# An encoder layer on one core: slots, orders at the seams, and own buffers for a head's first keys

## The chip, the cores and the metric

The kernel runs on one core of a Trainium2 chip. A core has the engines PE (matrix products), DVE, ACT and POOL (elementwise work) and SP, which here issues the DMAs. The metric is the device time of one execution in microseconds (us); less is better.

## The reference

One layer of a bidirectional encoder over 1024 positions of width 1024, in fp32:

```python
h   = rms_norm(x, g_pre)
z   = h @ W_in            # q, f_fwd, f_bwd, i, gate | u, v | two merge gates
A   = hgrn2(q, f_fwd, f_bwd, i) * silu(gate)     # 8 heads of 128 keys, both directions
Bm  = gelu(u) * (W_s @ layer_norm(gelu(v)) + b)  # per chunk of 128 positions
mix = (sigmoid(gate_a) * (A @ W_a) + sigmoid(gate_b) * (Bm @ W_b)) @ W_out
x   = x + rms_norm(mix, g_post)
x   = x + rms_norm(swiglu(rms_norm(x, g_ffn)), g_ffn_post)   # hidden width 2816
x   = x + (p @ W_ple) * sigmoid(x @ W_ple_gate)
```

In a head, S_t = diag(f_t) S_(t-1) + k_t v_t^T and o_t = S_t^T q_t, forward and backward, with f = lb + (1 - lb) sigmoid(zf) and k = (1 - lb) sigmoid(-zf).

## The kernel before

Every fp32 operand of a large product is split into a high and a low part (split_into: ACT writes the high part, DVE or POOL the low one), and each product is made in three passes (mm3, mm3c). A product on PE covers 128x512 of the output. Activations stay in SBUF with the features on the partitions; halves of 512 positions (n) are the unit.

The stages follow each other. First p @ W_ple (ple_product), while x is normalised and transposed to hT (norm_x, to_fm). Then four token-major groups (tm_group) make v, i and u, a spatial gate acts on u, and u is transposed to bT. branch_b multiplies w_b by bT, and beside it DVE forms the sums T1 to T4 of the four quarters of hT. These feed the class Seven, which makes a product of 2x2 blocks from seven block products (for the columns of q, gate and the merge, and later for the FFN's gate and up; begin makes the first two of the seven ahead). Then come the eight heads. For a head, proj multiplies two blocks of weights by hT and makes F (decays), X and Y (keys); scores goes through the levels m = 1, 2, 4, ..., 64. At each level PE makes scores of QA and X for both halves, DVE multiplies QA and X by F and puts the scores into SC (merge), and POOL renews Y; outputs chains the states S through the chunks on DVE and makes the head's output. The loop issues proj of the next head ahead of outputs of the current one. merge multiplies the heads' outputs by w_a, mix_half multiplies by W_out and normalises (y), and to_fm1 transposes for the FFN, which ends with down and the gated residual.

A scheduler with a timeline of its own sets each engine's order from the dependencies; the source order decides what it can see when. Each tile has a tag in a pool with a number of buffers, and an instruction that writes a buffer waits for the last readers of what was there. PSUM has eight banks under the tags mm (3), sc (2), tr, st and o. Loads are issued on SP in order, so a load whose buffer is not free holds those behind it.

## Time and profile before

| | |
|---|---|
| median of 3 runs | 1989.25 us (1988.0 to 1991.34) |
| profiled execution | 1992.11 us, span 1990.3 us |
| PE busy | 1926.7 us, 97% |
| DVE, ACT, POOL busy | 1106.0, 764.9, 208.5 us |
| mean granted clock of PE | 0.989 |

The span runs from the first to the last instruction of the trace. Busy time counts an engine's instructions; a product that runs at the lower clock counts as busy for longer. The stages by the trace: the start to 53 us, the other token-major groups to 229, the transposes of u and w_b's products to about 284, Seven's columns to about 560, the heads to 1037, the merge to about 1115, W_out and the norm to about 1220, the FFN and the end to 1990.

### The profile page before, as it was taken

How to read it: one execution, taken by the hardware profiler on the slowest of the kernel's cores; microseconds unless marked ns; L12 is line 12 of the kernel's file. 1: busy time of each engine (PE TensorE's matmuls, PEld its weight loads, DVE VectorE, ACT ScalarE, POOL GpSimd, SP SyncE). 2: the span in 40 equal slices, each digit the busy share in tenths (PEclk: the TensorE clock that was granted, in tenths of full speed). 3: DMA queues.
4: the chain of work that ended last, by engine and by line, in shares of the span. 5: the costliest groups of instructions: out<-in, count | busy, mean ns of one | idle time of the engine just before them, and what ended most of it. 6: DMA issues, size and time to landing. Idle time of an engine off the chain costs nothing.

```text
span 1990.3 us, 24039 instructions
## 1 busy us (share of the span) xinstructions
PE 1926.7 (97%) x9264; PEld 1604.8 (81%) x9264; DVE 1106.0 (56%) x1694; ACT 764.9 (38%) x1434; POOL 208.5 (10%) x153
## 2 busy tenths in 40 slices
PE   7999899999998999999999998999999999999999
PEld 6887788888887888888877886888888888888887
DVE  6401357545247777788754457855555536545743
ACT  7211244344344555445542146533333324213321
POOL 2600000000012222222112101000000000001000
PEclk9999899999999999999998998999999999999999
DMA  9120155433130112211336223232222205324232
GB/s 339 57 70 11 59 175 179 138 110 118 70 138 32 59 59 69 69 59 59 107 110 229 98 94 117 84 100 92 75 85 77 83 32 197 106 74 158 87 105 80
DMA packets 82147, 201.87 MB, mean 101 GB/s; under 512 B 8688, under 2 KB 17520, under 8 KB 82032
## 3 DMA queue, kind: packets, MB, share of 16 engines
q1 hardware_dynamic: 82032, 200.33, 30.0%
q8 instruction: 73, 1.20, 0.3%
q14 instruction: 42, 0.34, 0.1%
HBM read 147.35 MB, written 52.95 MB: 101 GB/s over the span
## 4 chain that ended last, share of the span: by engine, by line
PE 55%; DVE 5%; ACT 3%; issue 1%; DMA 1%; POOL 0%; DVEq 0%; SPq 0%; ACTq 0%; POOLq 0%
PE ps_mm L133 17%; PE ps_mm L280 12%; PE ps_sc L133 8%; PE ps_sc L280 6%; PE ps_st L133 4%; PE ps_sc L612 2%; DVE QA L621 1%; PE ps_tr L280 1%; PE ps_o L280 1%; PE ps_st L280 1%; DVE X L624 1%; PE ps_o L700 1%; DVE SC L634 1%; DVE F L654 1%; ACT SC L631 1%
## 5 line engine op out<-in xcount | busy, mean ns | idle before, releaser
L280 PE MATMUL ps_mm<-T,w 128*128 128x512 f32 x1296 | 310.1, 389 | 0.0
L280 PEld LDWEIGHTS ps_mm<-T,w 128*128 128x128 f32 x1296 | 243.2, 188 | 50.7 <-ACT u L230 0.2
L648 POOL TENSOR_TENSOR Y<-X,F 128x512 f32<-128x512 f32 x56 | 92.7, 1656 | 675.6 <-DVE F L587 401.8
L115 DVE TENSOR_TENSOR whl<-raw,whl 128x1024 fp32r<-128x1024 f32 (+1 forms) x70 | 85.5, 1225 | 132.0 <-ACT whl L114 132.0
L612 PE MATMUL ps_sc<-QA,X 128*128 128x128 f32 x896 | 125.5, 290 | 19.7 <-DVE QA L621 17.1
L115 DVE TENSOR_TENSOR w<-sums,w 128x1024 fp32r<-128x1024 f32 x72 | 88.1, 1223 | 92.8 <-ACT w L114 92.7
L612 PEld LDWEIGHTS ps_sc<-QA,X 128*128 128x128 f32 x896 | 115.1, 194 | 27.7 <-DVE QA L621 10.5
L133 PE MATMUL ps_mm<-whl,act 128*128 128x512 f32 x528 | 134.1, 389 | 0.0
L114 ACT ACTIVATE whl<-raw 128x1024 fp32r<-128x1024 f32 (+1 forms) x78 | 79.0, 1014 | 115.3 <-PE ps_sc L133 54.0
L133 PE MATMUL ps_mm<-hTa,whl 128*128 128x512 f32 x480 | 119.2, 396 | 0.0
L133 PE MATMUL ps_mm<-hTb,whl 128*128 128x512 f32 x480 | 117.8, 398 | 0.5 <-ACT F L580 0.5
L133 PEld LDWEIGHTS ps_mm<-whl,act 128*128 128x128 f32 x528 | 99.1, 188 | 20.7
L114 ACT ACTIVATE w<-sums 128x1024 fp32r<-128x1024 f32 x72 | 76.0, 1056 | 98.2 <-PE ps_sc L280 80.6
L280 PE MATMUL ps_sc<-T,w 128*128 128x512 f32 x432 | 108.5, 389 | 0.0
L621 DVE TENSOR_TENSOR QA<-QA,F 128x512 f32<-128x512 f32 x112 | 85.8, 767 | 34.1 <-PE ps_sc L612 33.5
L133 PEld LDWEIGHTS ps_mm<-hTb,whl 128*128 128x128 f32 x480 | 89.0, 189 | 18.7 <-ACT F L580 1.3
L133 PEld LDWEIGHTS ps_mm<-hTa,whl 128*128 128x128 f32 x480 | 88.4, 188 | 17.6 <-ACT F L580 0.2
L280 PEld LDWEIGHTS ps_sc<-T,w 128*128 128x128 f32 x432 | 81.1, 188 | 16.8
L133 PE MATMUL ps_sc<-whl,act 128*128 128x512 f32 x351 | 89.8, 390 | 0.0
L133 PEld LDWEIGHTS ps_sc<-whl,act 128*128 128x128 f32 x351 | 65.7, 188 | 13.8 <-ACT acc L927 0.2
L624 DVE TENSOR_TENSOR X<-X,F 128x256 f32<-128x256 f32 x112 | 74.6, 699 | 0.1
L645 ACT ACTIVATE X<-Y 128x512 f32<-128x512 f32 x56 | 36.1, 645 | 99.0 <-PE ps_sc L612 95.4
(311 smaller groups left out, 3566.7 us busy)
## 6 DMA issues: line engine op xcount, KB each, us to landing
raw<-in_w_fm_dram SPq DMA_DIRECT2D x52, 512.0 KB, 3.5
raw<-in_w_gate_dram SPq DMA_DIRECT2D x22, 512.0 KB, 3.4
raw<-in_w_up_dram SPq DMA_DIRECT2D x22, 512.0 KB, 3.9
act_d<-s SPq DMA_DIRECT2D x22, 512.0 KB, 2.9
raw<-in_w_down_dram SPq DMA_DIRECT2D x22, 512.0 KB, 3.8
raw<-act_d SPq DMA_DIRECT2D x22, 512.0 KB, 4.2
raw<-in_w_tm_dram SPq DMA_DIRECT2D x16, 512.0 KB, 5.6
pr_d<-h SPq DMA_DIRECT2D x16, 256.0 KB, 5.9
```

The lines of the kernel that those rows point to most:

```text
L114: nc.scalar.activation(hi, src, AF.Copy)
L115: (eng or nc.vector).tensor_tensor(out=lo, in0=src, in1=hi.bitcast(F32), op=ALU.subtract)
L133: nc.tensor.matmul(ps, lhsT=lhs(lp, k), rhs=rhs(rp, k), start=(i == 0), stop=(i == n - 1))
L280: nc.tensor.matmul(ps, lhsT=lhs(lp, k), rhs=rhs(rp, k), start=(first and i == 0), stop=(i == n - 1), skip_group_check=True)
L612: nc.tensor.matmul(sp[:, i * P:(i + 1) * P], lhsT=X[:, c * P:(c + 1) * P], rhs=view(QA, c * P, [[2 * m, cb], [T + m, 2], [1, m]]), start=T ...
L621: nc.vector.tensor_tensor(out=view(QA, o, qd), in0=view(QA, o, qd), in1=view(F, of + 1, [[nb - 1, 2], [2, nb // 4], [0, m]]), op=ALU.mult)
L624: nc.vector.tensor_tensor(out=view(X2, o, dims), in0=view(X, o, dims), in1=view(F, nb + of + 1, [[4, nb // 8], [1 - nb, 2], [0, m]]), op=A ...
L631: nc.scalar.activation(SC[p0:p0 + m, 4 * g:4 * g + 4, c0:c0 + m], sp.rearrange("p (c t) -> p c t", c=4)[p0:p0 + m, :, c0:c0 + m], AF.Copy)
L634: nc.vector.copy_predicated(SC[:, 4 * g:4 * g + 4], masks[:, li, None, :].broadcast_to([P, 4, P]), sp.rearrange("p (c t) -> p c t", c=4))
L645: nc.scalar.activation(view(X2, m, mid), view(Y, m, mid), AF.Copy)
L648: nc.gpsimd.tensor_tensor(out=view(Y, m, mid), in0=view(X, m, mid), in1=view(F, 0, [[4, nb // 4], [nb + 3, 2], [0, m]]), op=ALU.mult)
L654: nc.vector.tensor_tensor(out=F2, in0=Fv[:, :, :, 0], in1=Fv[:, :, :, 1], op=ALU.mult)
```

## The change

to_fm no longer keeps fp32 copies of hT (h32); the sums T are made from the high and low parts (sum_of), with 40 adds instead of 24. The pools raw and whl are open from the start and are used by the token-major groups as well, in place of p0r and two of p0w's six buffers. The first halves of pT and w_ple are loaded in four pieces, ahead of x. bT is made before the fourth token-major group, as a pair for each half. The first keys of a head have a tag of their own, X0, with two buffers; those of the levels keep X with three. In the merge, blocks 0 and 1 of w_a are split before the last head's outputs, and block j + 2 is loaded ahead of block j's products and split behind them. At the FFN the second products of the first two blocks get the banks st and sc.

```diff
@@ -157,8 +157,6 @@
-                if keep[g] is not None:
-                    nc.scalar.activation(keep[g][:, :, col * P:(col + 1) * P], tv, AF.Copy)
...
@@ -234,12 +232,12 @@
-        def begin(self, lhs, HB):
+        def begin(self, lhs, HB, bank):
...
             c11 = self.keep("p1", X)
-            Z = self.zbank()
+            Z = ps_tile(bank)
             self.add(lhs, HB, 2, Z, True)
...
@@ -289,15 +287,14 @@
     c_p01, p01 = phase("p01", side="right")
-    c_h32, p_h32 = phase("h32", side="right")
-    h32 = [[p_h32.tile([P, 4, NH], F32, name=f"h32_{n}{g}") if n == 0 or g == 1 else None for g in range(2)]
-           for n in range(2)]
+    c_x, p0x = phase("p0x", 3, side="right")
+    c_raw, rawp = phase("raw", 2)
+    c_whl, whlp = phase("whl", 2)
     c_sgu, sgu = phase("sgu")
     masks = p01.tile([P, len(LEVELS), P], U8, name="masks")
-    c_x, p0x = phase("p0x", 3)
-    c_r, p0r = phase("p0r", 3)
-    c_w, p0w = phase("p0w", 6)
-    c_t, p0t = phase("p0t", 2)
+    c_v, p0v = phase("p0v", 4)
+    c_w, p0w = phase("p0w", 4)
+    c_t, p0t = phase("p0t", 1)
...
@@ -313,16 +310,24 @@
-    praw = [p0w.tile([P, 2, 2, NH], F32, name="praw", tag="whl") for _ in range(2)]
+    praw = [whlp.tile([P, 2, 2, NH], F32, name="praw", tag="whl") for _ in range(2)]
...
-    load_pw(0, 0)
+    def piece(i, cut):
+        src, w, raw = a[("pT", "w_ple")[i]][0][:, cut[0], cut[1]], pwt[i][:, 0], praw[i][:, 0, cut[0], cut[1]]
+        nc.sync.dma_start(raw, src)
+        split_into(w[:, 0, cut[0], cut[1]], w[:, 1, cut[0], cut[1]], raw)
+    both, all_ = slice(0, 2), slice(0, NH)
+    piece(0, (both, slice(0, P)))
+    piece(1, (slice(0, 1), all_))
+    piece(1, (slice(1, 2), all_))
+    piece(0, (both, slice(P, NH)))
     load_x(0)
-    load_pw(1, 0)
     nc.sync.dma_start(ident, a["ident"])
...
@@ -368,7 +372,7 @@
-            s = t2(p0t, "vs", 2)
+            s = t2(p0v, "vs", 4)
...
@@ -378,7 +382,8 @@
-        return load_split(a["w_tm"][gi, kk], [2, NH], nc.gpsimd if kk % 2 else nc.vector, p0w, p0r)
+        pool = p0w if (4 * gi + kk) % 6 < 4 else whlp
+        return load_split(a["w_tm"][gi, kk], [2, NH], nc.gpsimd if kk % 2 else nc.vector, pool, rawp)
...
@@ -393,7 +398,7 @@
-        s = h32[1][1][:, t % 4]
+        s = t2(p0v, "vs", 4)
...
@@ -443,22 +450,20 @@
                                        op0=ALU.add, op1=ALU.mult)
+    c_b, p1b = phase("p1b", side="right")
+    bT = [pair(p1b, f"bT{n}", None) for n in range(2)]
+    for t in range(NT):
+        tp = ps_tile(("tr", "o")[t % 2])
+        for i in range(4):
+            nc.tensor.transpose(tp[:, i * P:(i + 1) * P], u[:, t, i * P:(i + 1) * P], ident)
+        ts = slice(t % 4 * P, (t % 4 + 1) * P)
+        split_into(bT[t // 4][0][:, :, ts], bT[t // 4][1][:, :, ts], tp.rearrange("p (k t) -> p k t", k=4))
     w = [load_tm(3, kk) for kk in range(4)]
     tm_group(w, ev_i(1))
-    close(c_t, c_w, c_r, c_x)
-    c_b, p1b = phase("p1b", side="right")
-    bT = [p1b.tile([P, 4, T], F32R, name=f"bT{p}") for p in range(2)]
-    for t in range(NT):
-        tp = ps_any()
-        for i in range(4):
-            nc.tensor.transpose(tp[:, i * P:(i + 1) * P], u[:, t, i * P:(i + 1) * P], ident)
-        split_into(bT[0][:, :, t * P:(t + 1) * P], bT[1][:, :, t * P:(t + 1) * P],
-                   tp.rearrange("p (k t) -> p k t", k=4))
+    close(c_w, c_v)
     close(c_sgu)
-    c_raw, rawp = phase("raw", 2)
-    c_whl, whlp = phase("whl", 2)
     c_T, Tp = phase("hT_T")
...
@@ -472,7 +477,7 @@
             ps = ps_any()
-            mm3(ps, lambda p, k: wb[:, p, k, :], lambda p, k: bT[p][:, k, n * NH:(n + 1) * NH], 4)
+            mm3(ps, lambda p, k: wb[:, p, k, :], lambda p, k: bT[n][p][:, k, :], 4)
             s = t2(p1t, "o", 2)
...
@@ -480,23 +485,30 @@
-    b11, b21, b22 = h32[0][0], h32[0][1], h32[1][1]
-    b12 = [hT[1][p][0].bitcast(F32) for p in range(2)]
+    b11, b21 = [[hT[0][p][g].bitcast(F32) for p in range(2)] for g in range(2)]
+    b12, b22 = [[hT[1][p][g].bitcast(F32) for p in range(2)] for g in range(2)]
+    def sum_of(out, terms):
+        acc, sign = terms[0]
+        for term, sign in terms[1:]:
+            nc.vector.tensor_tensor(out=out, in0=acc, in1=term, op=ALU.add if sign else ALU.subtract)
+            acc = out
     for k in range(4):
         sa, sb = [st1.sum_tile().rearrange("p a k c -> p a (k c)") for _ in range(2)]
-        nc.vector.tensor_tensor(out=sa[:, 0], in0=b12[0][:, k], in1=b11[:, k], op=ALU.subtract)
-        nc.vector.tensor_tensor(out=sa[:, 0], in0=sa[:, 0], in1=b12[1][:, k], op=ALU.add)
+        (b11h, b11l), (b12h, b12l), (b21h, b21l), (b22h, b22l) = [
+            [part[:, k] for part in blk] for blk in (b11, b12, b21, b22)]
+        sum_of(sa[:, 0], [(b12h, 1), (b11h, 0), (b12l, 1), (b11l, 0)])
         split_into(T1[0][:, k], T1[1][:, k], sa[:, 0])
-        nc.vector.tensor_tensor(out=sa[:, 1], in0=b22[:, k], in1=sa[:, 0], op=ALU.subtract)
+        sum_of(sa[:, 1], [(b22h, 1), (sa[:, 0], 0), (b22l, 1)])
         split_into(T2[0][:, k], T2[1][:, k], sa[:, 1])
-        nc.vector.tensor_tensor(out=sb[:, 0], in0=b22[:, k], in1=b12[0][:, k], op=ALU.subtract)
-        nc.vector.tensor_tensor(out=sb[:, 0], in0=sb[:, 0], in1=b12[1][:, k], op=ALU.subtract)
+        sum_of(sb[:, 0], [(b22h, 1), (b12h, 0), (b22l, 1), (b12l, 0)])
         split_into(T3[0][:, k], T3[1][:, k], sb[:, 0])
-        nc.vector.tensor_tensor(out=sb[:, 1], in0=b21[:, k], in1=sa[:, 1], op=ALU.subtract)
+        sum_of(sb[:, 1], [(b21h, 1), (sa[:, 1], 0), (b21l, 1)])
         split_into(T4[0][:, k], T4[1][:, k], sb[:, 1])
...
         branch_b(j)
-    close(c_b, c_h32)
+    close(c_b)
...
@@ -565,7 +577,7 @@
-                s.X = hg.tile([P, T], F32, name="X", bufs=3)
+                s.X = hg.tile([P, T], F32, name="X0", bufs=2)
...
@@ -723,6 +735,16 @@
+    def load_wa(j):
+        raw = rawp.tile([P, KD, P], F32, name="raw", tag="raw")
+        nc.sync.dma_start(raw, a["w_a"][j])
+        return raw
+    def split_wa(raw):
+        w = whlp.tile([P, 2, KD, P], F32R, name="whl", tag="whl")
+        split_into(w[:, 0], w[:, 1], raw)
+        return w
     def gate_a(n):
...
@@ -746,6 +768,7 @@
             A1 = new_fm("A1")
+            wa = [split_wa(load_wa(j)) for j in range(2)]
         outputs(h, cur)
...
@@ -761,17 +784,20 @@
         for j in range(KD):
-            w = load_split(a["w_a"][j], [KD, P], None, whlp, rawp)
+            if j + 2 < KD:
+                raw = load_wa(j + 2)
             for n in range(2):
...
                 ps = ps_any()
-                mm3(ps, lambda p, k: w[:, p, k, :], fm_rhs(A[n]), KD)
-                sg = t2(t3, "sg", 2)
+                mm3(ps, lambda p, k: wa[j][:, p, k, :], fm_rhs(A[n]), KD)
+                sg = t2(t3, ("sg", "xr")[n], 2)
                 nc.sync.dma_start(sg, sig_d[j, :, ns])
...
                 nc.vector.tensor_tensor(out=M[:, j, ns], in0=sg, in1=m0, op=ALU.add)
+            if j + 2 < KD:
+                wa.append(split_wa(raw))
             load_wo(j)
...
@@ -860,9 +886,9 @@
-    begun = [st4.begin(lhs, HB2)]
+    begun = [st4.begin(lhs, HB2, "st")]
...
-    begun.append(st4.begin(lhs1, HB2))
+    begun.append(st4.begin(lhs1, HB2, "sc"))
```

PE has as many instructions as before, ACT 10 fewer, DVE 18 more, SP 2 more. In the order of PE, at the end of the fourth token-major group, the kernel before has the transposes of u (ident, u) behind the group's last products (hTb), and w_b's products (bT) behind these:

```order
L133 MATMUL ps_sc<-whl,hTb_144 128x512 x2
L133 MATMUL ps_sc<-whl,hTb_146 128x512
L456 MATMUL ps_mm<-ident,u 128x128 x4
L456 MATMUL ps_st<-ident,u 128x128 x4
L456 MATMUL ps_mm<-ident,u 128x128 x4
L456 MATMUL ps_sc<-ident,u 128x128 x4
L456 MATMUL ps_mm<-ident,u 128x128 x4
L456 MATMUL ps_sc<-ident,u 128x128 x4
L456 MATMUL ps_mm<-ident,u 128x128 x4
L456 MATMUL ps_st<-ident,u 128x128 x4
L133 MATMUL ps_mm<-bT_1611,whl 128x512
L133 MATMUL ps_mm<-bT_1612,whl 128x512
```

In the changed kernel two tiles of u stand there in the middle of that group, in its first half of positions (hTa):

```order
L133 MATMUL ps_sc<-whl,hTa_146 128x512 x2
L133 MATMUL ps_sc<-whl,hTa_148 128x512
L133 MATMUL ps_sc<-whl,hTa_146 128x512
L458 MATMUL ps_tr<-ident,u 128x128 x4
L458 MATMUL ps_o<-ident,u 128x128 x4
L133 MATMUL ps_sc<-whl,hTa_146 128x512
L133 MATMUL ps_sc<-whl,hTa_148 128x512
L133 MATMUL ps_sc<-whl,hTa_146 128x512 x2
L133 MATMUL ps_sc<-whl,hTa_148 128x512
L133 MATMUL ps_mm<-whl,hTa_145 128x512 x2
L133 MATMUL ps_mm<-whl,hTa_147 128x512
```

The other transposes stand in the same way ahead of the group's end, and the last product of the group is followed at once by w_b's:

```order
L133 MATMUL ps_sc<-whl,hTb_150 128x512 x2
L133 MATMUL ps_sc<-whl,hTb_152 128x512
L133 MATMUL ps_sc<-whl,hTb_150 128x512 x2
L133 MATMUL ps_sc<-whl,hTb_152 128x512
L133 MATMUL ps_mm<-bT_1375,whl 128x512
L133 MATMUL ps_mm<-bT_1376,whl 128x512
L133 MATMUL ps_mm<-bT_1375,whl 128x512 x2
L133 MATMUL ps_mm<-bT_1376,whl 128x512
```

In the order of PE where a new head begins, the kernel before has, between the first scores (q, ks) and the level m=1 (QA, X), products of projections (hTa, whl):

```order
L601 MATMUL ps_sc<-q,ks 128x128 x8
L133 MATMUL ps_mm<-hTa_141,whl 128x512
L133 MATMUL ps_mm<-hTa_139,whl 128x512
L133 MATMUL ps_mm<-hTa_140,whl 128x512
L133 MATMUL ps_mm<-hTa_142,whl 128x512
L133 MATMUL ps_mm<-hTa_140,whl 128x512 x2
L133 MATMUL ps_mm<-hTa_142,whl 128x512
L133 MATMUL ps_mm<-hTa_140,whl 128x512 x2
L133 MATMUL ps_mm<-hTa_142,whl 128x512
L671 MATMUL ps_tr<-ident,X 128x128
L671 MATMUL ps_tr<-ident,Y 128x128
L671 MATMUL ps_tr<-ident,X 128x128
```

In the changed kernel no large product stands there, from the first scores to the first half of m=2; X and Y are transposed for the outputs of the head before, and v, kt make its states:

```order
L613 MATMUL ps_sc<-q,ks 128x128 x8
L683 MATMUL ps_tr<-ident,X 128x128
L683 MATMUL ps_tr<-ident,Y 128x128
L683 MATMUL ps_tr<-ident,X 128x128
L688 MATMUL ps_st<-v,kt 128x128 x4
L624 MATMUL ps_sc<-QA,X_4685 128x128 x4
L683 MATMUL ps_tr<-ident,X 128x128
L683 MATMUL ps_tr<-ident,Y 128x128
L683 MATMUL ps_tr<-ident,X 128x128
L624 MATMUL ps_sc<-QA,X_4685 128x128 x4
L688 MATMUL ps_st<-v,kt 128x128 x3
L624 MATMUL ps_sc<-QA,X 128x128 x4
```

The ten large products beside the first scores moved to other places.

In the order of SP around the merge, the kernel before loads the third block of w_a behind the loads of the gates (sig_d, m_d) and of x:

```order
L770 DMA sg<-sig_d 128x512
L772 DMA y<-m_d 128x512
L723 DMA xr<-at_d 128x512
L772 DMA y<-m_d 128x512 x2
L800 DMA xr<-in_x_dram 128x512 x2
L758 DMA gpost<-in_norm_mix_post_dram 128x1024
L770 DMA sg<-sig_d 128x512
L772 DMA y<-m_d 128x512
L120 DMA raw<-in_w_a_dram 128x1024
L770 DMA sg<-sig_d 128x512
L772 DMA y<-m_d 128x512
L779 DMA raw<-in_w_out_dram 128x1024
```

In the changed kernel three blocks of w_a are loaded ahead of the last stores of the heads' outputs (at_d):

```order
L120 DMA raw<-in_w_fm_dram 128x1024
L755 DMA sig_d<-sk 128x512
L740 DMA raw<-in_w_a_dram 128x1024
L755 DMA sig_d<-sk 128x512
L740 DMA raw<-in_w_a_dram 128x1024
L755 DMA sig_d<-sk 128x512
L740 DMA raw<-in_w_a_dram 128x1024
L755 DMA sig_d<-sk 128x512
L805 DMA raw<-in_w_out_dram 128x1024
L730 DMA at_d<-on 128x512
L735 DMA xr<-at_d 128x512 x5
L730 DMA at_d<-on 128x512
```

The third load moved from behind the merge's first gates to ahead of the last head's stores.

## Rows read from the trace of the kernel before

**Rows 1.** the page, part 1: busy us (share of the span) xinstructions

```profile
PE 1926.7 (97%) x9264; PEld 1604.8 (81%) x9264; DVE 1106.0 (56%) x1694; ACT 764.9 (38%) x1434; POOL 208.5 (10%) x153
```

**Rows 2.** timeline of PE from 225: start, us, line, operation, count, idle before

```profile
225.21 4.13 PE L133 MATMUL ps_sc<-whl,hTb 128*128 128x512 f32 x17
229.18 0.60 PE L456 MATMUL ps_mm<-ident,u 128*128 128x128 f32 x4
229.62 0.60 PE L456 MATMUL ps_st<-ident,u 128*128 128x128 f32 x4
...
239.20 1.22 PE L133 MATMUL ps_mm<-bT,whl 128*128 128x512 f32 x2 [3.43 <-ACT whl L114]
```

**Rows 3.** windows: length, busy us (xcount) by engine, PE clock, DMA share, GB/s

```profile
0.00:50.00 50.00, 39.00 (x179) 31.31 (x180) 33.34 (x56) 37.11 (x73) 12.70 (x16) 1.00 0.93 338
600.00:650.00 50.00, 43.24 (x255) 37.63 (x254) 37.11 (x63) 23.20 (x47) 11.65 (x7) 0.94 0.10 32
```

**Rows 4.** timeline of PE, the start

```profile
8.57 0.79 PE L133 MATMUL ps_mm<-wp,pT 128*128 128x512 f32 x1 [8.57 <-ACT wp L114]
...
40.42 1.88 PE L133 MATMUL ps_mm<-whl,hTa 128*128 128x512 f32 x7
```

**Rows 5.** timeline of ACT, the start

```profile
4.63 1.06 ACT L114 ACTIVATE pT<-praw 128x1024 fp32r<-128x1024 f32 x1 [2.61 <-DMA praw<-in_pT_dram]
```

**Rows 6.** timeline of SP's queue near 235

```profile
235.80 0.82 SPq L470 DMA_DIRECT2D raw<-in_w_b_dram  x2
```

**Rows 7.** timeline of DVE, the sums T

```profile
254.04 0.68 DVE L115 TENSOR_TENSOR T<-sums,T 128x512 fp32r<-128x512 f32 x1
254.65 0.68 DVE L115 TENSOR_TENSOR whl<-raw,whl 128x512 fp32r<-128x512 f32 x1
```

**Rows 8.** windows: a steady head, and stretches with a lower clock

```profile
702.60:755.64 53.04, 50.01 (x321) 44.12 (x320) 40.84 (x72) 27.78 (x73) 14.34 (x10) 1.00 0.20 65
640.00:650.00 10.00, 7.10 (x34) 6.16 (x33) 8.91 (x21) 3.85 (x8) 2.77 (x2) 0.72 0.17 52
1050.00:1060.00 10.00, 5.49 (x15) 3.63 (x15) 5.10 (x7) 1.89 (x2) 2.14 (x1) 0.70 0.79 250
1060.00:1070.00 10.00, 10.00 (x37) 7.99 (x35) 2.61 (x3) 2.34 (x3) 5.04 (x2) 0.79 0.72 231
1230.00:1235.00 5.00, 2.41 (x9) 2.04 (x10) 4.56 (x7) 2.16 (x8) 1.54 (x1) 0.50 0.55 180
1235.00:1240.00 5.00, 5.00 (x16) 3.92 (x16) 5.00 (x9) 3.38 (x6) 0.00 (x0) 0.67 0.62 192
```

**Rows 9.** groups of DVE in 702 to 756: count, busy us, mean ns, idle

```profile
L621 DVE TENSOR_TENSOR QA<-QA,F 128x512 f32<-128x512 f32 x14 | 10.9, 780 | 2.3 <-PE ps_sc L612 2.3
L624 DVE TENSOR_TENSOR X<-X,F 128x256 f32<-128x256 f32 x15 | 10.0, 695 | 0.0
L634 DVE COPY_PREDICATED SC<-masks,ps_sc 128x512 f32<-128x512 uint8 x11 | 8.0, 736 | 0.0
L682 DVE SCALAR_TENSOR_TENSOR S<-S,F,ps_st 128x128 f32<-128x128 f32 x13 | 4.4, 341 | 4.2 <-PE ps_st L676 4.1
```

**Rows 10.** lines L621 and L624: min/median/max ns, first and last start

```profile
L621 DVE TENSOR_TENSOR QA<-QA,F x112: 670/687/1499, 591.6 to 1021.8; 128x512 f32<-128x512 f32 x112
L624 DVE TENSOR_TENSOR X<-X,F x112: 402/416/2277, 582.3 to 1014.5; 128x256 f32<-128x256 f32 x112
```

**Rows 11.** timelines of DVE and POOL near 724

```profile
724.32 1.45 DVE L621 TENSOR_TENSOR QA<-QA,F 128x512 f32<-128x512 f32 x1
...
723.85 1.37 POOL L648 TENSOR_TENSOR Y<-X,F 128x512 f32<-128x512 f32 x1
```

**Rows 12.** timeline of SP's queue in the merge

```profile
1049.82 0.33 SPq L120 DMA_DIRECT2D raw<-in_w_a_dram  x1
```

**Rows 13.** timeline of PE, the waits in the merge and at the FFN

```profile
1055.55 1.22 PE L133 MATMUL ps_mm<-A,whl 128*128 128x512 f32 x2 [3.96 <-ACT whl L114]
...
1232.21 1.09 PE L820 MATMUL ps_tr<-ident,y 128*128 128x128 f32 x4 [6.94 <-DVE y L808]
```

More of the change, by code (lines that the diff above doesn't have):

```diff
@@ L145, in fm_lhs, with to_fm @@
         return lambda p, k: fm[p][k // 4][:, k % 4, col * P:(col + 1) * P]
-    def to_fm(fm, col, src, gvec, tags=("tr", "tr"), keep=None):
+    def to_fm(fm, col, src, gvec, tags=("tr", "tr")):
         for g in range(2):
@@ L349, in norm_x @@
         nc.vector.scalar_tensor_tensor(out=xt, in0=xt, scalar=r, in1=gmix, op0=ALU.mult, op1=ALU.mult)
-        to_fm(hT[t // 4], t % 4, lambda g: xt[:, g * NH:(g + 1) * NH], None, ("sc", "sc"),
-              keep=h32[t // 4])
+        to_fm(hT[t // 4], t % 4, lambda g: xt[:, g * NH:(g + 1) * NH], None, ("sc", "sc"))
     def ev_v(t, ps):
@@ L417 @@
             ple_product(e, t)
-    u, vn = [sgu.tile([P, NT, SGW], F32, name=name, tag="uv", bufs=2) for name in ("u", "vn")]
+    vn, u = [sgu.tile([P, NT, SGW], F32, name=name, tag="uv", bufs=2) for name in ("vn", "u")]
     def x_ahead(t):
@@ L435 @@
     nc.vector.tensor_copy(masks, mf)
+    close(c_x)
     tm_group(w, ev_i(0), layer_norm)
+    close(c_t)
     w = [load_tm(2, kk) for kk in range(4)]
```

## The prediction

> **What bounds the kernel now.** I read the busy times first: PE is busy 97% of the span, the next engine 56% [rows 1], so the time is the work of PE plus what PE loses. Then I asked how large that work is. On a stretch at the full clock 17 products of 128x512 start within 3.97 us (225.21 to 229.18), 0.233 us each, and behind them four small ones (128x128) every 0.44 us, 0.11 each [rows 2]. Counted over the whole program at such rates PE has about 1,890 us of work in a span of 1,990.3. Some 100 us are lost, and the change can touch only those, for it has as many products as before, of the same sizes.
>
> The next view is the span in windows of 50 us, in which the reader is to look for idle PE and for a granted clock below 1.00. The start (39.0 busy of the first 50) and the heads (43.2 in 600 to 650, clock 0.94) show it [rows 3]; three seams, near 235, 1050 and 1230, stand in finer rows below. Time at the lower of the two levels (1.2 GHz, read as 0.50 where a whole window lies in it) is half lost where PE is busy, so at each place I add the idle time and half of what ran at that level. The last view is the timeline of PE at those places, for what ends each wait.
>
> **The change, seam by seam.** The sums are made against the profiled execution (1992.1 us, 1.8 of it outside the span). It stands 2.9 above the median of 1989.25, and I take those 2.9 off at the end.
>
> *Start.* PE begins at 8.57 us, when w_ple is split, and the first token-major group begins at 40.42 [rows 4]. Until then PE has 96 products and 40 transposes, 96 x 0.233 + 40 x 0.11 = 26.8, so 13.6 are lost. ACT could begin on a piece of 512 KB at 4.63 [rows 5]. The change asks first for 128 KB of pT and 256 KB of w_ple, so I put the first product at about 5.3, 3.3 earlier; 18 of the 96 products now stand inside the group that follows, where they fill gaps; and 12 copies of ACT go. Against this, the DMA engines are busy to 0.93 over the first 50 us [rows 3] with the same bytes to bring, and the weights of the first group have two raw buffers instead of three. If the bytes decide, nothing is won; if PE's own work does, 7. I take 4, the middle, as both rows speak.
>
> *Transposes of u.* From 229.18 to 239.20 [rows 2] PE has 32 transposes, 3.5 us of work in 10.0: 6.5 lost, the last wait for w_b, whose load SP issues only at 235.80 [rows 6], when the spaces of the phase before are free. The products behind run at the lower level for some 6 us more, as they do behind the seam at 1230 (below): half of that, 2.8, makes 9.3. In the new order the transposes stand among the products of the fourth token-major group, the loads of w_b ahead of its last stores, and the first product of w_b right behind it. I take 8.5: 9.3 if PE waits for nothing there, 6 if it waits 3 for w_b. The cost is on DVE: the sums T1 to T4 take 40 adds instead of 24. DVE then has 40 adds, 16 splits of T and 8 of w_b, 64 x 0.68 = 43.5 us by whole durations [rows 7], beside 192 products of w_b, 44.7 us on PE. So they hide, but barely; with that cover gone the 16 added adds cost up to 16 x 0.68 = 10.9.
>
> *Heads.* A steady head takes 53.04 us with some 320 products [rows 8]. Its work is 96 x 0.233 + 224 x 0.11 = 47.0, so it loses 6.0, three of them idle. The old order has large products of a later head's projections beside a head's first scores; the new one puts all 96 large products between m=2 and m=16, and the run from m=16 to the first half of the next head's m=2 has none until just before its end. There DVE has 8 multiplications of QA, 4 merges, 8 halves of X, 8 steps of S and about 1.5 us of small ones. By the means of a steady head [rows 9] that is 8 x 0.78 + 4 x 0.736 + 8 x 0.695 + 8 x 0.341 + 1.5 = 19.0, less 0.07 by which each of some 30 overlaps the next (0.68 long, 0.61 apart [rows 7]): 16.9. With the first and the last scores (1.8) it is 18.7, against 14.5 of PE's work in the run: 4.2 lost, and 0.4 at m=8, so a cycle of 51.6. By the medians (0.687 for QA, 0.416 for X [rows 10]) DVE needs 13.9, and the cycle is 48.6. Were half of the QA as long as the one that began while POOL ran, 1.45 [rows 11], it would be 51.6 + 4 x 0.67 = 54.3, 1.3 more than now. I take 52.0, nearest to the means: 1.04 won in each of five cycles, 5.2. Head 0 loses more: 600 to 650 has 6.8 idle and a clock of 0.94 [rows 3], some 9.4 where a steady head loses 5.6. Its new order has 41 products of the next projections behind m=4, 9.6 us of filler, of which I take 5.7, since the levels before m=4 still wait. Between heads 6 and 7 the products of gate_a fill the run: 3 of the 6. The last head now waits where those products stood, 1 lost, and 1 more goes to w_a, which holds a raw buffer meanwhile. Together 5.2 + 5.7 + 3 - 2 = 11.9, 12. The two buffers for a head's first keys count only through this order: ACT may write them before the keys of the levels are free. The bounds are 27 won (cycles of 48.6 to 49.0) and 20 lost (the first rival).
>
> That DVE waits on POOL is in the rows: a QA with a mean of 0.78 took 1.45 at 724.32, while POOL's product ran from 723.85 to 725.22 [rows 11]. The Trainium skill (SBUF — State Buffer, "SBUF: two separate sides") says that GpSimd and a DVE operation with two SBUF inputs contend for one pair of ports, held by one of them for a whole instruction; this trace agrees. By that rule the cycle would go toward 54.3, as POOL's four products of the run have no pause of DVE to fall into; without it, toward 48.6.
>
> *Merge.* SP issues the third block of w_a at 1049.82 [rows 12], and PE waits 3.96 for it up to 1055.55 [rows 13]. The ten microseconds from 1050 have 4.5 idle, and the clock's 0.70 and 0.79 in the two windows from 1050 [rows 8] are 6.0 and 4.2 us at the lower level; 8.1 of these are busy, 4.1 lost: 8.6 in all. In the new order that load stands ahead of the last head's stores. I take 7.5 (8.6 for no wait; 5 if the block after it is late by 3.6). The wait for the last head's outputs, just before, stays.
>
> *FFN.* PE waits 6.94 up to 1232.21 for y [rows 13]; 1230 to 1235 runs at 0.50 with 2.4 busy and the next five at 0.67 [rows 8], 1.2 and 1.65 lost. That is 9.8. In the new order 24 more products (24 x 0.233 = 5.6 us) stand ahead of the last transposes, on banks that are free. But two adds on DVE and ACT's copies for them now stand ahead of y, which I take to be 1 to 2 later. Won 5.5, with 2 and 8 for y later by 4 and for no delay.
>
> Sum: 4 + 8.5 + 12 + 7.5 + 5.5 = 37.5. 1992.1 - 37.5 - 2.9 = 1951.7, so 1952.
>
> **The rivals.** *The run in the heads lowers the clock.* By the order and the durations above PE idles in it 1.0, 1.1 and up to 2.4 at a time, with small products between. For it: in 640 to 650, with 2.9 idle, the clock was 0.72 [rows 8], 5.6 us at the lower level, 2.8 lost. Against it: a steady cycle has 3.0 idle and keeps 1.00 [rows 8]. If each of six runs paid those 2.8 and half a microsecond of wait, the heads would lose 20 instead of gaining 12: 25.5 - 20 = 5.5 won, 1984. The Trainium skill (TensorE: Matmul & The Clock Gate, "A second HAM failure mode: psum-queue depth-cycling") speaks for it: in a kernel that cycled through its accumulation banks PE idled briefly between groups, and its clock went down and up. The steady cycle does not agree with it, the window at 640 does.
>
> *The heads run through.* If POOL's products fall between DVE's, the heads gain 27: 25.5 + 27 = 52.5, 1937. For it speaks that the median of QA is 0.687; against it, that DVE has no pause there.
>
> *Seams come back as later waits.* The T sums are late, since ACT, which copies each of them, also empties the banks of w_b's products, and the start is held by its bytes. With 5 of the 10.9 paid, nothing won at the start and 3 less at merge and FFN together, 12 of the 37.5 go: 1964.
>
> *Slower.* The same run stays at the lower level from m=16 to m=2: its 14.5 of work takes 29, a cycle 47.0 + 14.5 = 61.5, 8.5 longer than now. Over seven seams that is 60 lost, less the 25.5 of the others: 34 slower, 2024. It decides from 25.5 / 7 = 3.6 us a seam, somewhat over what 640 to 650 lost by the clock. Against it: behind today's seams at 1050 and 1230 PE is back at full speed within some ten microseconds, with large products, as stand behind m=2 here.
>
> **How the numbers follow.** The forecast has 0.50, the heads that run through 0.15, later waits 0.15, the lowered clock 0.14, the slower case 0.06. The range leaves out the slower case and a part of the heads that run through; it reaches 4 below that case's time and just takes in the lowered clock: 1932 to 1985. Executions of this kernel differ by 0.2%, 4 us, so less can't be told from no change. The lowered clock lies 5 below the median; I count 0.05 of it as no change and 0.01 as slower, so faster 0.87, same 0.06, slower 0.07.
>
> **What would show it.** Right: the first product near 5.3 us; no wait above 2 between the fourth token-major group and w_b's products, with the clock at 1.00 there; the wait for w_a gone; a wait for y below 3.5; steady heads of 51.5 to 52.5. Wrong: a clock below 0.9 in each head; a head over 53.0; a wait of the first columns for T or their weights; a first token-major group later than 37. If the heads take as long as now, the forecast fails in its most uncertain term, and the time is about 1964.

## The result, and the profile after

The changed kernel takes 1968.43 us (median of 4 runs, 1966.99 to 1968.68) and the kernel before 1988.62 beside it (4 runs, 1987.39 to 1991.34). The ratio is 0.9895, with a 95% interval of 0.9878 to 0.9912: faster by 1.05%, or 20.2 us. The forecast was 1952, 36.6 faster than that run of before.

The profiled execution took 1966.99 us and its span is 1965.2, 25.1 shorter than that of before. The profiled execution of before lay 3.5 above its median and this one 1.4 below, which is why the medians differ by 4.9 less. PE's line of the page (busy us, share of the span, instructions) answers to [rows 1]:

```profile
PE 1910.8 (97%) x9264; PEld 1596.0 (81%) x9264; DVE 1120.0 (57%) x1712; ACT 757.2 (39%) x1424; POOL 206.7 (11%) x153
```

PE is busy 15.9 us less with the same products, which is time at the lower clock that went (mean granted clock 0.989 before, 0.997 after); another 9.2 of idle time went. The windows (us; length, busy us by engine, clock, DMA share, GB/s) answer to [rows 3, 8]:

```profile
0.00:50.00 50.00, 40.06 (x181) 31.27 (x182) 34.42 (x53) 30.29 (x59) 13.41 (x15) 1.00 0.80 294
600.00:650.00 50.00, 45.22 (x284) 40.10 (x283) 41.22 (x70) 23.52 (x47) 10.96 (x7) 1.00 0.11 34
729.46:782.31 52.85, 49.01 (x320) 43.95 (x319) 40.52 (x72) 27.59 (x71) 14.01 (x10) 1.00 0.20 66
1030.00:1040.00 10.00, 8.24 (x36) 6.18 (x35) 8.10 (x9) 1.91 (x2) 2.40 (x1) 1.00 0.62 215
1040.00:1050.00 10.00, 10.00 (x46) 8.28 (x45) 3.91 (x5) 2.12 (x2) 2.39 (x1) 1.00 0.71 260
1210.00:1220.00 10.00, 8.29 (x27) 6.16 (x26) 9.23 (x14) 5.33 (x12) 0.00 (x0) 0.66 0.37 115
```

The clock stands at 1.00 in the head at 600 and in the merge from 1030 on. It still falls where PE has waited: behind the last outputs of the heads (0.85 from 1020 to 1030, 0.83 from 1037 to 1047 in the kernel before) and behind the seam at 1210. The third row is a steady head: 52.85, where it was 53.04.

To see where the time came from I add up the work of all products in PE's order at one rate for each size (some 1,890 us, the same in either kernel) and take it, at marks of the program, from the time in the trace. What is left is lost up to that mark. The two columns of lost time hang on these rates; what is won hardly does, as both kernels have the same products. In us between two marks:

| stretch | lost before | lost after | won | predicted |
|---|---|---|---|---|
| start, to the second half of the first token-major group | 13.6 | 12.6 | 1.0 | 4 |
| transposes of u, w_b, Seven's columns | 15.2 | 5.4 | 9.8 | 8.5 |
| heads, to the last transposes of outputs | 53.4 | 47.3 | 6.1 | 12 |
| merge, to the first product of W_out | 8.8 | 2.3 | 6.5 | 7.5 |
| W_out, FFN and end | 5.5 | 3.7 | 1.8 | 5.5 |
| sum | | | 25.2 | 37.5 |

The timeline of PE (start, us, line, operation, count, idle before and its releaser) shows the places of [rows 2, 4, 13]:

```profile
5.86 3.23 PE L133 MATMUL ps_mm<-wp,pT 128*128 128x512 f32 x6 [5.86 <-ACT wp L114]
34.37 1.65 PE L133 MATMUL ps_mm<-wp,pT 128*128 128x512 f32 x6 [2.17 <-DVE vs L405]
35.86 4.83 PE L133 MATMUL ps_mm<-whl,hTa 128*128 128x512 f32 x20
...
225.55 5.76 PE L133 MATMUL ps_sc<-whl,hTb 128*128 128x512 f32 x24
231.15 2.96 PE L133 MATMUL ps_mm<-bT,whl 128*128 128x512 f32 x12
...
1209.30 0.63 PE L846 MATMUL ps_tr<-ident,y 128*128 128x128 f32 x4 [2.81 <-DVE y L834]
1212.08 1.22 PE L278 MATMUL ps_mm<-B,wA 128*128 128x512 f32 x2 [1.71 <-ACT wA L114]
```

The first product of w_b follows the group without a pause. The wait for y is 2.81 instead of 6.94, but a wait of 1.71 for the weights wA stands behind it. The heads hold the largest miss. In the seam of a steady head the timelines of POOL, DVE, ACT and PE have these rows:

```profile
727.19 4.13 POOL L660 TENSOR_TENSOR Y<-X,F 128x512 f32<-128x512 f32 x1 [3.37 <-ACT X L657]
...
728.87 0.75 DVE L636 TENSOR_TENSOR X<-X,F 128x256 f32<-128x256 f32 x2
729.54 1.83 DVE L666 TENSOR_TENSOR F<-F 128x32 f32<-128x32 f32 x1
731.29 0.28 DVE L692 COPY S<-ps_st 128x128 f32<-128x128 f32 x1
...
731.35 0.67 ACT L657 ACTIVATE X<-Y 128x512 f32<-128x512 f32 x1 [2.17 <-POOL Y L660]
732.04 0.60 ACT L685 ACTIVATE kt<-ps_tr 128x512 f32<-128x512 f32 x1
...
732.69 0.33 PE L683 MATMUL ps_tr<-ident,X 128*128 128x128 f32 x1 [1.28 <-ACT kt L685]
```

POOL makes the next head's product Y of m=1 (128x256x2) beside DVE's run and takes 4.13 for it; 56 such products of all levels have a median of 1.31 here. DVE's F operation on 128x32 takes 1.83 and ends with POOL's product. ACT's copy X<-Y waits for POOL, the keys kt stand behind that copy, and PE waits for kt.

### The profile page after: what moved, and what is told of

It is laid out like the page before. It is cut to its first block, busy times and chain, and to the rows that moved or that the text cites. A ratio compares the mean times of both kernels' runs of the same rounds, so it can differ in the third digit from the quotient of the medians.

```text
span 1965.2 us, 24005 instructions
## 1 busy us (share of the span) xinstructions
PE 1910.8 (97%) x9264; PEld 1596.0 (81%) x9264; DVE 1120.0 (57%) x1712; ACT 757.2 (39%) x1424; POOL 206.7 (11%) x153
## 4 chain that ended last, share of the span: by engine, by line
PE 90%; DVE 4%; ACT 2%; DMA 2%; POOL 1%; issue 1%; SPq 0%; DVEq 0%; POOLq 0%; ACTq 0%
PE ps_mm L133 29%; PE ps_mm L278 20%; PE ps_sc L133 11%; PE ps_sc L278 10%; PE ps_st L133 6%; PE ps_sc L624 4%; PE ps_o L278 2%; PE ps_o L712 2%; PE ps_tr L278 2%; PE ps_st L278 1%; DVE QA L633 1%; POOL Y L660 1%; PE ps_st L688 1%; ACT SC L643 0%; DMA raw<-in_w_gate_dram 0%
## 5 line engine op out<-in xcount | busy, mean ns | idle before, releaser
L115 DVE TENSOR_TENSOR whl<-raw,whl 128x1024 fp32r<-128x1024 f32 (+1 forms) x70 | 89.6, 1282 | 142.7 <-ACT whl L114 142.6
L624 PE MATMUL ps_sc<-QA,X 128*128 128x128 f32 x896 | 126.4, 288 | 16.9 <-DVE QA L633 16.9
L624 PEld LDWEIGHTS ps_sc<-QA,X 128*128 128x128 f32 x896 | 116.1, 192 | 26.1 <-DVE QA L633 19.0
L633 DVE TENSOR_TENSOR QA<-QA,F 128x512 f32<-128x512 f32 x112 | 91.8, 828 | 49.2 <-PE ps_sc L624 48.1
L133 PE MATMUL ps_mm<-hTa,whl 128*128 128x512 f32 x480 | 115.1, 392 | 0.0
L278 PEld LDWEIGHTS ps_sc<-T,w 128*128 128x128 f32 x432 | 81.1, 188 | 16.9
L115 POOL TENSOR_TENSOR wpg<-raw,wpg 128x1024 fp32r<-128x1024 f32 x4 | 9.6, 2403 | 598.3 <-ACT wpg L114 593.6
L278 PE MATMUL ps_mm<-B,wA 128*128 128x512 f32 x264 | 67.3, 399 | 1.7 <-ACT wA L114 1.7
```

What stands on the lines that cost most here:

```text
L115: (eng or nc.vector).tensor_tensor(out=lo, in0=src, in1=hi.bitcast(F32), op=ALU.subtract)
L133: nc.tensor.matmul(ps, lhsT=lhs(lp, k), rhs=rhs(rp, k), start=(i == 0), stop=(i == n - 1))
L278: nc.tensor.matmul(ps, lhsT=lhs(lp, k), rhs=rhs(rp, k), start=(first and i == 0), stop=(i == n - 1), skip_group_check=True)
L624: nc.tensor.matmul(sp[:, i * P:(i + 1) * P], lhsT=X[:, c * P:(c + 1) * P], rhs=view(QA, c * P, [[2 * m, cb], [T + m, 2], [1, m]]), start=T ...
L633: nc.vector.tensor_tensor(out=view(QA, o, qd), in0=view(QA, o, qd), in1=view(F, of + 1, [[nb - 1, 2], [2, nb // 4], [0, m]]), op=ALU.mult)
```

## The experiments

All are made from the changed kernel. Times are medians of 4 or 5 runs (11 for Y on DVE); ratios stand to the kernel before on the same chip, 1987.97 to 1989.51 there. Differences to the changed kernel (1968.43, timed beside its own runs of the kernel before) are taken between medians; by the ratios they come out up to 1.3 us otherwise. In the groups of rows the timeline has the columns of [rows 2], windows those of [rows 3].

**The two buffers alone taken back** (x_shared).

```
-                s.X = hg.tile([P, T], F32, name="X0", bufs=2)
+                s.X = hg.tile([P, T], F32, name="X", bufs=3)
```

> The changed kernel with the two buffers X0 taken back: a head's first keys share the tag X again. Time of the changed kernel: 1968.4, the kernel before 1988.6. Theory (the buffers let the scheduler write the next head's keys m=1 to 4 in the seam, and the 6 us that the heads gained come from that order alone): the start, the transposes of u, the merge and the FFN keep their gains, the heads give 6 back, 1974 to 1975, and a steady head takes 53.0 to 53.1. Rival (the heads' gain comes from the other edits, which give the planner other times): within 2 of the changed kernel, 1967 to 1970, a steady head of 52.8.

1975.84, ratio 0.993 (0.9916 to 0.9943), 7.4 slower. A steady head is that of before again:

```profile
737.26:790.32 53.06, 50.04 (x320) 44.14 (x319) 40.82 (x72) 27.73 (x71) 14.34 (x10) 1.00 0.20 65
```

From the first scores to the last output it loses 53.7, as before (53.4). All that the heads gained comes from the two buffers. The theory holds. In this execution, the slowest of the five, 4 more are lost in the merge, where PE waits 3.02 for the split of w_a.

**Y of m=1 (and m=2) on DVE** (y1_dve, y12_dve).

```
-            nc.gpsimd.tensor_tensor(out=view(Y, m, mid), ...
+            (nc.vector if m == 1 else nc.gpsimd).tensor_tensor(out=view(Y, m, mid), ...
```

> The changed kernel with one product moved: Y of the level m=1 (128x256, twice a head) is made on DVE instead of POOL. In the changed kernel this product took 4.13 us on POOL (727.19 to 731.32) where the others take 1.1 to 1.5; ACT's next X waits 2.17 for it, the keys kt behind it on ACT, and PE idles 1.28. Theory A (POOL is starved by DVE's run of operations with two SBUF inputs, and its late Y holds ACT and PE): a steady head loses that 1.28 and a part of the QA waits behind it, 51.0 to 51.6, eight heads 10 to 14 in all, 1955 to 1960. Rival B (DVE's own run sets the seam, and two more operations of 0.3 to 0.5 lengthen it): a steady head of 53.4 to 53.8 and 1972 to 1976.

> The changed kernel with Y of the levels m=1 and m=2 on DVE instead of POOL. Theory A (POOL's products in the seam are what holds it): as with m=1 alone or 2 to 4 better, 1952 to 1960; DVE's operations beside them at 0.2 to 0.7 instead of up to 1.83. Rival B (DVE's run sets the seam): 0.8 to 1.4 more in each head, 1975 to 1980.

1991.80 (ratio 1.001, 1.0002 to 1.0019) and 1991.31 (1.0009, 1.0000 to 1.0018): 23 slower, which neither theory had. The scheduler gave PE another order in the heads. Heads 1 to 6 of the first take 53.6, 54.4, 50.3, 49.7, 55.0 and 58.0. A head of 55.0, and the last head, in windows:

```profile
831.44:886.44 55.00, 50.60 (x320) 44.89 (x319) 41.21 (x73) 27.81 (x71) 11.12 (x9) 0.97 0.19 63
944.44:1043.12 98.68, 82.75 (x509) 72.99 (x508) 47.27 (x89) 36.63 (x117) 13.29 (x12) 0.94 0.26 86
```

The last head loses 24 where it lost 10. These runs say nothing of POOL's product; they say that what an edit does to the order can outweigh what it does to an operation.

**The product left out, the order kept** (y1_none), **and with one input** (y1_ts).

```
-            nc.gpsimd.tensor_tensor(out=view(Y, m, mid), ...
+            m > 1 and nc.gpsimd.tensor_tensor(out=view(Y, m, mid), ...         # y1_none
+            nc.gpsimd.tensor_scalar(out=..., in0=view(X, m, mid), scalar1=0.75, ...) if m == 1 else ...   # y1_ts
```

> The changed kernel without POOL's product Y of the level m=1: it leaves that multiplication by F out (eight of POOL's 56 products), and Y keeps its old value there. The orders of PE, DVE and SP stay as they are, so that this run tells what the product costs where the move to DVE could not, since that gave PE another order. Theory A (POOL's 4.13 us product holds ACT's X, kt and then PE): the 1.28 of PE's wait for kt goes from each of the steady heads, and a part of the 1.0 behind it, so a steady head of 51.0 to 51.7 where the changed kernel has 52.85, and 1956 to 1961. Rival B (the DVE run sets the seam, and what is won at kt is waited for at the next QA): a steady head of 52.5 to 52.9, and 1965 to 1968.5.

> The changed kernel with POOL's product Y of the level m=1 by a constant instead of by F: it leaves F out there, so that the operation has one input in SBUF instead of two. All orders stay as they are. Theory (POOL is starved only where its operation and DVE's both read two inputs from SBUF): it takes 1.0 to 1.5 in the seam instead of 4.13, and the time comes as without the product, 1956 to 1962. Rival (any operation of POOL is held up beside DVE's run): it takes 3 to 4.2 there, and the time stays at 1966 to 1969.

Without the product 1958.04, ratio 0.9849 (0.9835 to 0.9862), 10.4 faster. With one input 1964.73, 0.9883 (0.9870 to 0.9897), 3.7 faster. First the window of a steady head without the product, and from its timelines DVE's F operation and PE's first transpose, now without a wait:

```profile
729.49:780.84 51.35, 48.79 (x320) 43.93 (x319) 38.89 (x72) 27.84 (x72) 9.88 (x8) 1.00 0.19 67
```

```profile
729.57 0.18 DVE L666 TENSOR_TENSOR F<-F 128x32 f32<-128x32 f32 x1
729.67 0.28 DVE L692 COPY S<-ps_st 128x128 f32<-128x128 f32 x1
...
731.27 0.27 PE L683 MATMUL ps_tr<-ident,X 128*128 128x128 f32 x1
```

Then the timeline of the same place with one input:

```profile
725.95 3.90 POOL L660 TENSOR_SCALAR Y<-X 128x512 f32<-128x512 f32 x1 [3.37 <-ACT X L657]
...
728.29 0.67 DVE L666 TENSOR_TENSOR F<-F 128x32 f32<-128x32 f32 x1
...
731.22 0.33 PE L683 MATMUL ps_tr<-ident,X 128*128 128x128 f32 x1 [1.06 <-ACT kt L685]
```

The product costs 1.5 us in each of four steady heads, 1.9 in the head before them and 1.1 at the last seams, 9.0 in all: theory A. PE's order is that of the changed kernel, and in the steady head the wait of 1.28 for kt is the only one that goes; those for QA (0.46, 1.02, 0.67 and 0.17) stay. The F operation takes 0.18 without it. With one input POOL is held up nearly as long (3.90, as the rival said), but it holds DVE for 0.49 instead of 1.65. The time lies between the two forecasts: the four steady heads take 52.6, only 0.2 less each, since kt still waits, and the head before them takes 51.4 as without the product. The Trainium skill (SBUF — State Buffer, "SBUF: two separate sides") says that an operation of DVE with two inputs in SBUF contends with any of GpSimd that reads SBUF; the 3.90 of an operation with one input agrees.

**The copy moved to POOL** (xc2_pool). ACT's X<-Y of m=2 goes to POOL, so that kt no longer stands behind it.

```
+            nc.gpsimd.tensor_copy(view(X2, m, mid), view(Y, m, mid)) if m == 2 else nc.scalar.activation(...)
```

> The changed kernel with one copy moved: ACT's X<-Y of the level m=2 is made by POOL, behind its product Y of m=1 for which the copy waits. Nothing is left out, and the orders of PE, DVE and SP stay as they are. Theory (the loss is ACT's queue: the keys kt stand behind a copy that waits for POOL): POOL's product still takes 3.9 to 4.2 us, but kt no longer waits for it, PE's wait of 1.28 goes, a steady head of 51.3 to 51.8, and 1957 to 1962, as much as without the product (1958). Rival (DVE is what PE waits for, as its F operation is held up to the end of POOL's product, 1.83 us, and POOL's two operations more in a row hold it up again): kt is on time but the wait comes back at S or QA, a steady head of 52.3 to 52.9, and 1965 to 1969.

1970.82, ratio 0.9909 (0.9893 to 0.9924): nothing won. My theory fell, and the time lies just above the rival's 1965 to 1969. Steady heads take 52.43 and 53.07 by turns. kt is on time, but PE now waits for DVE:

```profile
732.12 1.84 DVE L666 TENSOR_TENSOR F<-F 128x32 f32<-128x32 f32 x1
733.89 0.28 DVE L692 COPY S<-ps_st 128x128 f32<-128x128 f32 x1
...
735.72 1.16 PE L688 MATMUL ps_st<-v,kt 128*128 128x128 f32 x8 [1.41 <-DVE S L694]
```

Two strands hold PE there, ACT's queue and DVE's F operation, and both end with POOL's product.

**The merge's loads as before** (wa_old).

```
-            wa = [split_wa(load_wa(j)) for j in range(2)]
+            wa = {j: load_split(a["w_a"][j], [KD, P], None, whlp, rawp)}      # at block j's turn
```

> The changed kernel with the merge weights w_a loaded and split as in the kernel before, each block at its own turn. Theory (the 6.6 us that the merge gained are this edit's): a wait of 3 to 5 for a block of w_a comes back near 1035 to 1050 with a clock below 0.85 behind it, and 1973.5 to 1976. Rival (the merge gained because the heads end in another order): 1967.5 to 1970.

1978.15, ratio 0.9950 (0.9938 to 0.9963), 9.7 slower. SP issues a block of w_a behind thirteen loads of outputs, gates and constants, and PE waits longer than in the kernel before (9.25 against 3.96):

```profile
1036.44 0.43 SPq L120 DMA_DIRECT2D raw<-in_w_a_dram  x1
...
1043.36 1.22 PE L133 MATMUL ps_mm<-A,whl 128*128 128x512 f32 x2 [9.25 <-ACT whl L114]
```

The theory holds in its cause; the price is above its 3 to 5. The edit is worth more than the 6.5 that the merge gained, because without it the merge would have got worse: this load goes out 16.4 behind the last transposes of outputs, 12.4 in the kernel before. Why it goes out later is not shown.

**The transposes of u behind the group** (bt_late): the loop over t stands behind `tm_group(w, ev_i(1))` again.

> The changed kernel with the transposes of u behind the fourth token-major group again, while the pools stay open and w_b is loaded early. Theory (both the order and the early load were needed, each for about half): no wait for w_b, but 3 to 4 us of idle PE at the 32 transposes and a clock below 1.00 behind them, 4 to 6 lost, 1972.5 to 1974.5. Rival 1 (the early load alone was worth it): within 2, 1967 to 1970. Rival 2 (the order alone): all 9.3 come back, 1977 to 1978.

1975.52, ratio 0.9935 (0.9923 to 0.9948), 7.1 slower: between theory and rival 2. PE does not wait for w_b, but for the copies of the transposes, and the clock falls. Rows of PE's timeline, then a window behind them:

```profile
231.68 0.66 PE L460 MATMUL ps_tr<-ident,u 128*128 128x128 f32 x4 [1.30 <-DVE bT L115]
232.88 1.01 PE L460 MATMUL ps_o<-ident,u 128*128 128x128 f32 x4 [0.54 <-DVE bT L115]
234.58 1.22 PE L133 MATMUL ps_mm<-bT,whl 128*128 128x512 f32 x2 [0.69 <-ACT bT L114]
```

```profile
235.00:240.00 5.00, 5.00 (x17) 4.12 (x17) 4.01 (x7) 1.19 (x2) 0.00 (x0) 0.51 0.01 3
```

The order is worth some 7 of the 9.8. The rest would be the early load of w_b, which was not taken back by itself.

**The FFN's banks of before** (banks_old), **and the root on ACT** (rr_act).

```
-    begun = [st4.begin(lhs, HB2, "st")]        # banks_old: "tr"; the second, "sc", becomes "o"
-        nc.gpsimd.tensor_tensor(out=r, in0=v, in1=expo[:, 0:w], op=ALU.pow)     # rr_act, last row tile:
+        nc.scalar.activation(r, v, AF.Sqrt), eng.reciprocal(out=r, in_=r)
```

> The changed kernel with the FFN's banks of before: the second products of the first two blocks of Seven share the banks tr and o with the transposes. Theory (the banks are what the FFN gained, 1.8 us): the wait for y is 5 to 7 instead of 2.8 and the clock behind it falls further, 1970 to 1972. Rival (the FFN gained from the other edits, or its loss is set by the weights wA): within 1 of the changed kernel, 1967.5 to 1969.5.

> The changed kernel, but the reciprocal root of the last row tile's norm ahead of the FFN is made by ACT (square root) and DVE (reciprocal) instead of POOL (power). There POOL's operation on 128x1 took 2.60 us (1205.97 to 1208.57) where it takes 0.54 elsewhere, and PE waits 2.81 for y behind it and then 1.71 for the weights wA. Theory (POOL's starved operation is in the chain of y): y comes 1.5 to 2 earlier, the wait for y falls to 1 or less, and of this at most 1 is won since wA then ends last: 1967 to 1968. Rival (the chain of y is late for another reason, or the table that ACT loads for the root costs as much, some 1.3 twice): the wait for y stays at 2.5 to 4, 1968 to 1970.

With the old banks 1972.41, ratio 0.9920 (0.9906 to 0.9933): 4.0 slower by the medians and 1.7 by the time lost in the FFN of its trace; how much of the rest is the start's spread (below) stays open. The wait for y is that of before:

```profile
1209.92 1.09 PE L846 MATMUL ps_tr<-ident,y 128*128 128x128 f32 x4 [6.94 <-DVE y L834]
```

With the root on ACT 1969.76, ratio 0.9901 (0.9888 to 0.9915), no gain. ACT has two more loads of a table than in the changed kernel, and PE has y's transposes behind the products of wA, so the wait for y does not show. ACT's rows, then PE's:

```profile
1208.57 1.28 ACT L101 ACT_TABLE_LOAD   x1
1209.87 0.20 ACT L101 ACTIVATE rr<-rv 128x1 f32<-128x1 f32 x1
...
1211.03 1.28 ACT L908 ACT_TABLE_LOAD   x1
...
1213.00 1.06 ACT L114 ACTIVATE wA<-raw 128x1024 fp32r<-128x1024 f32 x1
...
1214.11 1.22 PE L278 MATMUL ps_mm<-B,wA 128*128 128x512 f32 x2 [5.64 <-ACT wA L114]
```

The two rows of the changed kernel that answer to it are these:

```profile
1208.68 0.87 DVE L834 TENSOR_SCALAR y<-y,rr 128x512 f32<-128x512 f32 x2
...
1210.97 1.06 ACT L114 ACTIVATE wA<-raw 128x1024 fp32r<-128x1024 f32 x1 [1.54 <-DMA raw<-in_w_gate_dram]
```

The time is the rival's, the wait for y is not. In the changed kernel DVE had no idle time before y, which began 0.11 behind the end of POOL's slow root (2.60, to 1208.57), so its trace does not show that the root held y up. In this run the root is no earlier, and y begins 7.0 behind DVE's last sum for that root (L110), where it began 4.9 behind it. And PE's product of wA comes as late as in the changed kernel, 5.6 behind the end of the products before the seam. In the changed kernel ACT waits there for wA's load from DRAM. What a faster root alone would give is not shown; while wA comes when it does, the time that y leaves goes to the wait for wA.

**The first loads whole** (start_old): pT and w_ple in halves as before, x between them; the pools stay as changed.

```
-    piece(0, (both, slice(0, P)))
...
+    load_pw(0, 0)
     load_x(0)
+    load_pw(1, 0)
```

> The changed kernel with the first loads of before: the first half of pT and of w_ple whole, with x between them, instead of in four pieces. Theory (the start gained 1.5 in the profiled execution, of which the pieces are the greater part): the first product at 8.3 to 8.7 instead of 5.9, the first token-major group 1 to 2 later, 1969.5 to 1970.5. Rival 1 (the start is held by its bytes): the group begins when it did, 1967.5 to 1969. Rival 2 (the 4 of the prediction): 1972 to 1973.

1963.99 (1963.66 to 1965.22), ratio 0.9879 (0.9865 to 0.9893): 4.4 faster than the changed kernel (3.2 by the ratios), and the fastest that computes all. The intervals of the ratios overlap, the single runs do not (1966.99 is the lowest of the changed kernel). Neither theory nor rivals had a gain. PE starts later and reaches the first token-major group 2.4 earlier than in the changed kernel's trace, for it does not wait again:

```profile
9.21 0.79 PE L133 MATMUL ps_mm<-wp,pT 128*128 128x512 f32 x1 [9.21 <-ACT wp L114]
...
32.00 1.64 PE L133 MATMUL ps_mm<-wp,pT 128*128 128x512 f32 x6
33.48 4.83 PE L133 MATMUL ps_mm<-whl,hTa 128*128 128x512 f32 x20
```

The pieces stand ahead of x, whose first two tiles land at 8.47 and 9.14 in the changed kernel and at 5.39 and 6.76 here. The changed kernel then waits five times from 15 to 35 us, 4.1 in all and each time for DVE. How much of these waits is x and how much DVE's order was not told apart. Of the 3.3 between the two traces 1.9 are won in the first stretch of the table; 1.1 more are won behind the merge, which this edit does not touch.

**Both strands loosened, with the whole loads** (f_early).

```
+        Fs = [F]
+        for m in LEVELS:        # all halvings of F ahead of the levels; bufs=2 from m=8 on
+            F2 = ...
+            Fs.append(F2)
...
```

> A version that should beat both kernels: the changed kernel with the first loads of before (1964.0 by itself), ACT's copy X<-Y of m=2 on POOL, and the chain of F of a head (seven halvings on DVE) made ahead of its levels, the small ones with two buffers, so that no product of F stands on DVE behind the run at the seam. Nothing is left out, and PE's order in the heads is the same but for a product or two. Theory (two strands held PE there: ACT's queue, where kt stood behind a copy that waits for POOL, and DVE's F operation, which POOL's product held up to its end, 1.84 us; taking away one alone gave nothing, and both go here): POOL's product still takes about 4, the first S copy follows the run at once, kt is on time, a steady head of 51.2 to 51.7 as without the product (51.36), and 1952 to 1957. Rival (POOL holds up whatever stands next on DVE, the S copies too): a steady head of 52.3 to 52.9 and 1962 to 1966.

1974.82, ratio 0.9935 (0.9921 to 0.9949): 10.8 slower than with the whole loads alone. Both theory and rival fell: the four steady heads take 54.1 to 54.8, and nearly all that is lost is lost in the heads. The timelines of POOL, DVE and PE in the seam:

```profile
783.17 2.50 POOL L660 TENSOR_TENSOR Y<-X,F 128x512 f32<-128x512 f32 x1 [3.36 <-ACT X L657]
785.73 1.00 POOL L656 COPY X<-Y 128x512 f32<-128x512 f32 x1
786.81 1.56 POOL L660 TENSOR_TENSOR Y<-X,F 128x512 f32<-128x512 f32 x1
...
783.31 2.91 DVE L632 TENSOR_TENSOR QA<-QA,F 128x512 f32<-128x512 f32 x2
786.14 2.51 DVE L635 TENSOR_TENSOR X<-X,F 128x256 f32<-128x256 f32 x2
788.57 0.28 DVE L689 COPY S<-ps_st 128x128 f32<-128x128 f32 x1
...
790.05 1.55 PE L685 MATMUL ps_st<-v,kt 128*128 128x128 f32 x8 [2.35 <-DVE S L691]
```

Now POOL gets its turn earlier (2.50) and DVE pays within the run: 2.91 for a pair that takes 1.28, and 2.51 for one that takes 0.75. POOL's product falls on the QA, and its next one, behind the copy, on the X. In these rows each product takes 1.6 to 1.8 from DVE (1.65 of the F operation in the changed kernel), and here two of them fall into the run. Two edits were made at once, so which of them moved POOL's turn, and what decides at which of DVE's operations POOL gets it, is not shown.

## Why the prediction was right or wrong

*Transposes of u* (8.5): right, 9.8 won, no wait, clock 1.00, and the sums T were not late (PE has no wait from 240 to 560). *Merge* (7.5): right, 6.5; one wait of 1.74 is left, for a split on DVE.

*Heads* (12): the step that failed, 6.1 won. Its terms by the marks: the cycles of heads 2 to 5 won 1.4 together, three of them 0.2 each, where 1.04 a cycle (4.2) was written; heads 0 and 1 won 6.8 (5.7 and one cycle of 1.04, 6.7); the seam of 6 and 7 2.1 (3); the last head lost 4.1 (2 with w_a). Of the 5.9 that are missing 2.8 are the steady cycles, 0.9 the seam and 2.1 the last head, where PE now waits 1.33 for the outputs A and 1.48 for QA, which it did not in the kernel before. For the run I had 16.9 by DVE's means and a cycle of 51.6, and had noted that POOL's products beside it would bring it toward 54.3; I took 52.0. With one of POOL's products left out a head takes 51.35, close to the 51.6; but that is no test of the working by DVE's means, since the means hold part of POOL's delays already, and POOL's other products are still there. What was mis-sized is POOL. I priced it as DVE's operations being slower, half of the QA by 0.67. In fact the QA of the run stayed at their length (1.28 a pair) and POOL was held off, for 4.13 instead of 1.3; the wait came through ACT, whose keys stood behind a copy that waits for POOL, and through one operation of F (1.83 instead of 0.18). An engine that I had costed only as a disturber was itself in the chain. Of my signs, the steady heads of 51.5 to 52.5 failed by this, at 52.85.

*Start* (4): 1.0 by the trace, which is the best start of eleven (last section), and by start_old the pieces lost 3.2 to 4.4. I had counted the earlier first product (3.3; it came 2.7 earlier) and not what was moved behind it: x. With the whole loads the other edits won some 3 there, 13.6 lost before and 10.7 in start_old; these are single traces, and the pools and the dropped copies were not told apart. *FFN* (5.5): 1.8. The wait for y fell as said (2.81, below 3.5), and y itself was no later; but the 1.71 for wA behind it, whose load comes late, was not in the sum, and the clock still fell to 0.66 for ten microseconds.

*The rivals.* The run does not lower the clock: the steady cycle has 3.8 us idle at 1.00. The heads did not run through. "Seams come back as later waits" (1964) came nearest to the time, and the start did win next to nothing, as it said; but the rest of its mechanism did not come: the T sums and the merge were on time. The slower case did not come.

Of the 16.4 by which the time was missed, 12.3 are these terms; the other 4 are the spread of executions. The forecast took the whole sum off a profiled execution and then 2.9 more to come to the median; the traces differ by 25.1, but the medians only by 20.2, as the profiled execution of before lay above its median and the one after 1.4 below.

*A slip.* The prediction's work of 1,890 does not come from its own rates: 7,264 products at 0.233 and 2,000 at 0.11 are 1,912, which leaves 78 lost and not 100. Back to back the medians in the trace are 0.227 and 0.112, which gives 1,873. No term of the sum is taken from this total.
